# All pairs of the MLPs' odd steps in seven products, two hidden tiles in one buffer, four blocks split by one operation

## The chip, the cores and the metric

The kernel runs on one core of one Trainium2 chip. The metric is the device time of one execution in microseconds, the median of the runs. The engines of the core are named as in the profile: PE (TensorE), with PEld for its weight loads, DVE (VectorE), ACT (ScalarE), POOL (GpSimd) and SP (SyncE, which here only starts the loads of the weights).

## What is computed

A trunk of two layers on a sequence of 256 tokens with 2048 channels, in float32. Layer 0 mixes tokens by a gated short convolution, layer 1 by a stick-breaking attention, and each is followed by an MLP with squared ReLU and 8192 hidden channels:

```
def sq_relu_mlp(u, w_up, w_down):
    return jnp.square(jax.nn.relu(u @ w_up)) @ w_down
...
        u = rmsnorm(h, mlp_pre_g[i])
        h = h + rmsnorm(sq_relu_mlp(u, mlp_w_up[i], mlp_w_down[i]), mlp_post_g[i])
```

The change lies in the two MLPs alone.

## The kernel before

**Numbers in two parts.** A float32 matrix is split into a rounded part (`whi`, `hi`, made by ACT with a copy) and the rest (`wlo`, `lo`, made by DVE with a subtraction), and a product of two such matrices is three matmuls: hi by hi, hi by lo, lo by hi. Weights come from HBM in chunks of 128x1024 float32 (512 KB, tile `raw`, five buffers, loaded by SP's queue one after the other). `chunk(i)` hands out the parts of chunk `i` and first splits all chunks up to `i + 4` (`AHEAD`), so that ACT and DVE work about four chunks ahead of PE. Each part lies in a ring of seven buffers (`RING`).

**Steps and units.** The hidden channels of an MLP are taken in eight steps of 1024 channels, which are eight tiles of 128 channels by 256 tokens (`Hidden(e)`, tiles `n` = 0 to 7, pairs `m` = 0 to 3). In step `e` the kernel computes the hidden tiles of step `e + 1` (`whole_up`, two chunks for each) and multiplies the tiles of step `e` by their rows of the second matrix (`Down.pair`, two chunks for each). One tile up and one pair down take turns; together they are called a unit here, four chunks. A step has eight units: four (`h` = 0) in which the pairs 0, 1, 2, 3 meet one half of the output columns, four (`h` = 1) in which the pairs 1, 2, 3, 0 meet the other half. PE's order is written out by hand; the orders on DVE and ACT are the scheduler's, fixed when the kernel is built.

**Eight products and seven.** A pair down is a product of a 2 by 2 block matrix of the activations (two blocks of 128 tokens, two tiles) with a 2 by 2 block matrix of weights (two chunks, each with two halves of 512 columns). `eight` does it in eight products of 128x512, 24 matmuls, on the two chunks as they are. `seven` does it in seven products, 21 matmuls, by Winograd's form of Strassen's scheme. It needs four sums of the weight blocks (`split_seven`: four DVE subtractions of 128x512 into `sums`, line L210, and then the split into parts of `b11`, of the second chunk, and of two tiles with the sums: names `wloNa` with 512 columns, `wloNb`, `wloNt`, `wloNu` with 1024, N being the chunk's number) and four sums of the activation blocks (`Hidden.sums_of`). The table `SEVEN` says which pairs of a step take seven products: in even steps all four, in odd steps (1, 3, 5) the pairs 1, 2 and 3, and in step 7 only pair 0 in the first half. So pair 0 of an odd step takes eight products, once in each half.

**A hidden tile.** When PE has finished a tile in PSUM, ACT copies one half out (`half`), DVE adds the other (`s<-up,half`, L966, high priority), and ACT applies ReLU and square in place. Before, each tile has a buffer of its own. In a pair that takes seven products, the first tile's first token block is split, then the whole second tile, then the sum `s1`, then the other three sums together (`more`, tag `hg`, five buffers): four copies on ACT and four subtractions on DVE, next to the four sums (`four_sums`, L271) in the tile `sq`, which has one buffer. A pair that takes eight products has both tiles split whole, and the difference of the two token blocks (`dif`) made and split, tile by tile.

The outputs of the products gather in PSUM over all the pairs of a plan; at the plan's end three banks are added by DVE to `mg` (L1073, three operations of 128x512), four are copied out by ACT and added by DMAs that POOL starts (`mg<-more`, L1033).

Of the kernel before, what the change touches and what calls it, by code (L numbers as in the profile page):

```python
# [9 lines left out]
F32 = mybir.dt.float32  # L10
F32R = mybir.dt.float32r
AF = mybir.ActivationFunctionType
ALU = mybir.AluOpType

P = 128
D = 2048
T = 256
NB = T // P
# [28 lines left out]
STEPS = 8  # L47
# [1 line left out]
UP_BANK = 2  # L49
DOWN_BANKS = {(0, 0): 3, (0, 1): 4, (1, 0): 5, (1, 1): UP_BANK, 1: 6, 5: 7, 6: 0, 7: 1}  # L50
LAST_BANKS = [[6, 7], [0, 1]]
SEVEN = [((0, 1, 2, 3),) * 2 if e % 2 == 0 else ((1, 2, 3),) * 2 for e in range(STEPS - 1)] + [((0,), ())]
ORDER = ((0, 1, 2, 3), (1, 2, 3, 0))

IN_N = [j * KD + i for i in range(KD) for j in range(3)]
# [40 lines left out]
def trunk(ctx, tc, x, xT, vecs, rows, ws, out):  # L96
    nc = tc.nc
# [45 lines left out]
    raw, parts, early = {}, {}, {}  # L143
# [109 lines left out]
    def split_tile(xs, k, src):  # L253

        hi, lo = xs[k // 4][:, k % 4, 0, :, :], xs[k // 4][:, k % 4, 1, :, :]
        src = src.rearrange("p (b t) -> p b t", b=NB)
        nc.scalar.activation(hi, src, AF.Copy)
        nc.vector.tensor_tensor(lo, src, hi.bitcast(F32), op=ALU.subtract)
# [7 lines left out]
    def four_sums(to, a11, a21, a12, a22):  # L266
        s1, s2, s3, s4 = to
        for t, v, w, op in (
            (s1, a21, a22, ALU.add), (s2, s1, a11, ALU.subtract), (s3, a11, a21, ALU.subtract), (s4, a12, s2, ALU.subtract),
        ):  # L270
            nc.vector.tensor_tensor(t, v, w, op=op)  # L271
# [25 lines left out]
    def spent(us):  # L297
        clock["us"] += us
        while due and due[0][0] <= clock["us"]:
            heappop(due)[2]()  # L300
# [622 lines left out]
    with tc.tile_pool(name="p_in", bufs=1, reuse_waits="tile") as tmp:  # L923
        y = convolution(tmp)
# [14 lines left out]
    def mlp(pool, i, before, after):  # L939
        u = before.x4  # L940
        part = [[None] * 4 for _ in range(NB)]
        held = {}
        scale = [None] * NB

        def two_parts(parts, src):
            hi, lo = parts
            nc.scalar.activation(hi, src, AF.Copy)
            nc.vector.tensor_tensor(lo, src, hi.bitcast(F32), op=ALU.subtract)

        class Hidden:  # L950


            def __init__(self, e):
                self.xs, self.sums = [None] * (NF // 4), {}
                first, second = SEVEN[e]
                self.pairs = [2 * m for m in first]
                self.apart = [2 * m for m in first if m not in second]
                self.eights = [2 * m for m in range(4) if m not in first] if e < STEPS - 1 else []

            def x(self, n, b):  # L960
                return [part_of(self.xs, n, b, j) for j in range(2)]

            def tile(self, n, ps, half):
                s = pool.tile([P, T], F32, tag="s", name="s", bufs=3)
                with tc.high_priority():
                    nc.vector.tensor_tensor(s[:], ps[:, :T], half[:], op=ALU.add)  # L966
                nc.scalar.activation(s[:], s[:], AF.Relu)  # L967
                nc.scalar.activation(s[:], s[:], AF.Square)
                if self.xs[n // 4] is None:
                    self.xs[n // 4] = operand("hid4")  # L970
                if n in self.pairs and n not in self.apart:
                    two_parts(self.x(n, 0), s[:, :P])
                else:
                    split_tile(self.xs, n, s[:])
                if n in self.pairs:
                    held[n] = s
                elif n - 1 in self.pairs:
                    self.sums[n - 1] = self.sums_of(n - 1, held.pop(n - 1), s)
                elif n - n % 2 in self.eights:
                    if n % 2 == 0:  # L980
                        self.sums[n] = pool.tile([P, 2, 2, P], F32R, tag="d", name="sums", bufs=1)
                    parts = [self.sums[n - n % 2][:, n % 2, j, :] for j in range(2)]
                    d = pool.tile([P, P], F32, tag="dif", name="dif", bufs=1)
                    nc.vector.tensor_tensor(d[:], s[:, :P], s[:, P:], op=ALU.subtract)
                    two_parts(parts, d[:])

            def sums_of(self, n, x, y):

                t = after.dump()
                four_sums([t[:, j * P : (j + 1) * P] for j in range(4)], x[:, :P], x[:, P:], y[:, :P], y[:, P:])  # L990
                if n in self.apart:
                    one = pool.tile([P, 2, 2, P], F32R, tag="d", name="sums", bufs=1)
                    one = [one[:, 0, j, :] for j in range(2)]
                else:
                    one = self.x(n, 1)
                more = pool.tile([P, 6 * P], F32R, tag="hg", name="sums", bufs=5)
                more = [more[:, j * 3 * P : (j + 1) * 3 * P] for j in range(2)]
                two_parts(one, t[:, :P])
                two_parts(more, t[:, P:])
                return [one] + [[m[:, j * P : (j + 1) * P] for m in more] for j in range(3)]  # L1000

        pss, adds = {}, []
# [103 lines left out]
        class Down:  # L1106


            def __init__(self, j, plan):
                self.j, self.plan, self.ps = j, plan, {}  # L1110
                sevens_at = [at for at in plan if at[1] in SEVEN[at[0]][at[2]]]
                whole_at = [at for at in plan if at not in sevens_at and at[0] == STEPS - 1]
# [41 lines left out]
            def eight(self, at, first, xs, n):  # L1154
                ws = [chunk(first + t) for t in range(2)]

                def products(key, own, x, c):
                    self.products(key, own, at, [
                        (x(t), [w[:, c * HALF : (c + 1) * HALF] for w in ws[t]]) for t in range(2)
                    ])  # L1160

                products((0, 0), "sum", lambda t: xs.x(n + t, 0), 0)
                products((1, 0), "sum", lambda t: xs.x(n + t, 1), 0)
                if at[0] == STEPS - 1:
                    products((0, 1), "sum", lambda t: xs.x(n + t, 0), 1)
                    products((1, 1), "whole", lambda t: xs.x(n + t, 1), 1)
                else:
                    products((0, 1), "sum", lambda t: [xs.sums[n][:, t, j, :] for j in range(2)], 1)
                    products(5, "fifth", lambda t: xs.x(n + t, 1), 1)
                spent(4 * UNIT)  # L1170

        for e in range(STEPS):
            for h in range(2):
                for m in SEVEN[e][h]:
                    n = 16 * h + 4 * ORDER[h].index(m) + 2 if e < STEPS - 1 else 8 * h + 2 * m
# [3 lines left out]
        for e in range(STEPS):  # L1179
            first = W["mlp", i, e + 1].base  # L1180
# [303 lines left out]
```

## Time and profile before

| | |
|---|---|
| median of 3 runs (lowest to highest) | 2108.14 us (2107.08 to 2108.43) |
| the profiled execution | 2106.03 us, of which the span from first to last instruction is 2104.3 us |
| granted TensorE clock in it | 0.998 |
| PE busy | 99% of the span |
| DVE busy | 87% |
| ACT busy | 68% |
| chain that ended last | PE 96%, DVE 3% |
| weights `raw<-w_mlp` | 512 issues of 512 KB, 4.7 us each from issue to landing (median) |

In the page a group row gives line, engine, operation, output and input tiles, shapes and count, then the busy time in us and the mean duration in ns, then the idle time of the engine ahead of these instructions. A row of the timeline begins with start and duration in us. A windows row gives, for a stretch of time, the busy time of each engine with its count of instructions, the granted clock, the share of the DMA engines' time and the rate. The steps of the first MLP run from 406 to about 988 us, those of the second from 1470 us on.

### The profile page before, as it was taken

The numbers are of one execution on the slowest core, as the hardware profiler recorded it, in microseconds if no ns is written. First come the engines' busy times: TensorE is split into PE (matmuls) and PEld (weight loads), VectorE is DVE, ScalarE is ACT, GpSimd is POOL, SyncE is SP. The second block draws the span as 40 slices with busy tenths as digits, with TensorE's granted clock in tenths as the row PEclk, the third lists the DMA queues.
The fourth block names the chain that finished last, engine by engine and source line by source line (L and its number), as shares of the span: only waits on it lengthen the run. The fifth ranks groups of instructions, "written<-read, shape, count | busy, mean of one in ns | idle before, by whom it ended". The sixth has DMA issues, their size and how long they took to land.

```text
span 2104.3 us, 29885 instructions
## 1 busy us (share of the span) xinstructions
PE 2089.1 (99%) x10608; PEld 1782.1 (85%) x10608; DVE 1837.6 (87%) x2807; ACT 1437.4 (68%) x2210; POOL 112.9 (5%) x137
## 2 busy tenths in 40 slices
PE   9999999999999999999999999999999999999998
PEld 7888888888888888888888888889888888888886
DVE  8999965999899999999766777558999999999997
ACT  8666544776776776767567888547867767677673
POOL 0000000000100101001000000000001010010010
PEclk9999999999999999999999999999999999999999
DMA  8467674577878868779575555655687687786784
GB/s 291 151 205 250 196 258 143 187 234 229 233 220 233 248 204 244 229 228 257 180 224 168 160 160 161 220 179 171 187 254 227 217 248 221 228 253 208 231 241 162
DMA packets 132342, 449.23 MB, mean 213 GB/s; under 512 B 14816, under 2 KB 15072, under 8 KB 131168
## 3 DMA queue, kind: packets, MB, share of 16 engines
q1 hardware_dynamic: 113184, 406.55, 60.1%
q0 software_dynamic: 18720, 40.38, 9.5%
q8 instruction: 83, 1.36, 0.3%
q14 instruction: 67, 0.55, 0.1%
q10 hardware_dynamic: 288, 0.39, 0.1%
HBM read 413.19 MB, written 2.10 MB: 197 GB/s over the span
## 4 chain that ended last, share of the span: by engine, by line
PE 96%; DVE 3%; issue 0%; DMA 0%; ACT 0%; SPq 0%; DVEq 0%; ACTq 0%
PE up L1013 21%; PE up L1020 12%; PE acc L326 8%; PE acc L328 8%; PE acc L327 8%; PE acc L748 5%; PE more L1127 5%; PE more L1126 5%; PE more L1128 5%; PE acc L1126 5%; PE acc L1127 4%; PE acc L1128 4%; PE lead L748 1%; PE up L1015 1%; PE tr L263 1%; DVE wlo L184 1%
## 5 line engine op out<-in xcount | busy, mean ns | idle before, releaser
L184 DVE TENSOR_TENSOR wlo<-raw,whi 128x1024 fp32r<-128x1024 f32 (+1 forms) x442 | 528.2, 1205 | 96.0 <-ACT whi L173 91.0
L173 ACT ACTIVATE whi<-raw 128x1024 fp32r<-128x1024 f32 (+1 forms) x442 | 454.5, 1044 | 172.8 <-PE acc L328 81.8
L1013 PE MATMUL up<-u,whi 128*128 128x512 f32 x1952 | 464.9, 389 | 0.0
L1013 PEld LDWEIGHTS up<-u,whi 128*128 128x128 f32 x1952 | 365.0, 188 | 74.7
L1020 PEld LDWEIGHTS up<-u,wlo 128*128 128x128 f32 x2048 | 263.6, 191 | 10.3
L1020 PE MATMUL up<-u,wlo 128*128 128x256 f32 x2048 | 268.1, 283 | 0.0
L186 DVE SCALAR_TENSOR_TENSOR wlo<-raw,gv,whi 128x512 fp32r<-128x512 f32 (+1 forms) x160 | 131.8, 854 | 41.4 <-ACT whi L173 40.7
L210 DVE TENSOR_TENSOR sums<-raw,sums 128x512 f32<-128x512 f32 x236 | 161.6, 685 | 1.3
L173 ACT ACTIVATE whi<-raw,gv 128x512 fp32r<-128x512 f32 (+1 forms) x160 | 121.7, 801 | 48.3 <-PE acc L328 41.9
L326 PE MATMUL acc<-whi,u 128*128 128x512 f32 x384 | 153.1, 399 | 0.1
L328 PE MATMUL acc<-whi,u 128*128 128x512 f32 x384 | 149.9, 390 | 0.0
L327 PE MATMUL acc<-wlo,u 128*128 128x512 f32 x384 | 149.7, 390 | 0.0
L1033 POOL DMA_DIRECT2D mg<-more x108 | 94.2, 872 | 829.9 <-ACT more L1088 425.3
L1026 ACT ACTIVATE half<-up 128x256 f32<-128x256 f32 x128 | 48.7, 382 | 99.3 <-PE up L1020 96.2
L748 PE MATMUL acc<-u,whi 128*128 128x512 f32 x416 | 98.9, 391 | 2.7 <-DVE sum L757 2.7
L748 PEld LDWEIGHTS acc<-u,whi 128*128 128x128 f32 x416 | 77.4, 188 | 20.5 <-DVE sum L757 3.7
L210 DVE TENSOR_TENSOR sums<-raw,raw 128x512 f32<-128x512 f32 x118 | 80.8, 685 | 13.8 <-DMA raw<-w_mlp 13.8
L210 DVE TENSOR_TENSOR sums<-raw 128x512 f32<-128x512 f32 x118 | 80.8, 685 | 5.7 <-DMA raw<-w_mlp 5.3
L328 PEld LDWEIGHTS acc<-whi,u 128*128 128x128 f32 x384 | 72.1, 188 | 15.5
L967 ACT ACTIVATE s<-s 128x256 f32<-128x256 f32 x128 | 52.3, 412 | 47.2 <-DVE s L966 45.9
L326 PEld LDWEIGHTS acc<-whi,u 128*128 128x128 f32 x384 | 72.2, 188 | 13.9 <-ACT tk L1316 0.6
L327 PEld LDWEIGHTS acc<-wlo,u 128*128 128x128 f32 x384 | 72.3, 188 | 13.2
(5995 smaller groups left out, 4508.4 us busy)
## 6 DMA issues: line engine op xcount, KB each, us to landing
raw<-w_mlp SPq DMA_DIRECT2D x512, 512.0 KB, 4.7
raw<-w_in SPq DMA_DIRECT2D x94, 512.0 KB, 4.4
mg<-more POOLq DMA_DIRECT2D x108, 256.0 KB, 6.5
raw<-w_out SPq DMA_DIRECT2D x32, 512.0 KB, 4.5
raw<-w_v SPq DMA_DIRECT2D x32, 512.0 KB, 4.4
raw<-w_k SPq DMA_DIRECT2D x32, 512.0 KB, 4.4
raw<-w_q SPq DMA_DIRECT2D x32, 512.0 KB, 4.3
raw<-w_wo SPq DMA_DIRECT2D x32, 512.0 KB, 3.7
```

What stands on the lines that cost most here:

```text
L173: rounded = nc.scalar.activation(hi[:, at], raw[i][:, at], AF.Copy, scale=1.0 if gain is None else gain)
L184: nc.vector.tensor_tensor(lo[:, at], t[:, at], hi[:, at].bitcast(F32), op=ALU.subtract)
L210: nc.vector.tensor_tensor(t, x, y, op=ALU.subtract)
L326: nc.tensor.matmul(ps[:], xh, hi[:, a], start=i == 0 and k == 0, stop=False)
L327: nc.tensor.matmul(ps[:], xh, lo[:, a], start=False, stop=False)
L328: nc.tensor.matmul(ps[:], xl, hi[:, a], start=False, stop=i == self.n - 1 and k == self.ks - 1)
L748: nc.tensor.matmul(ps[:, :cols], w, xs[:, :cols], start=k == 0 and part == parts[0], stop=k == KD - 1 and part == parts[1], skip_group_che ...
L1013: nc.tensor.matmul(ps, weight(0, first, m), x, start=k == 0, stop=False)
L1020: nc.tensor.matmul(pss[n][:, :T], weight(1, first, m), x, start=False, stop=k == KD - 1)
L1126: nc.tensor.matmul(self.ps[key][:], xh, hi, start=first, stop=False)
L1127: nc.tensor.matmul(self.ps[key][:], xh, lo, start=False, stop=False)
L1128: self.done = nc.tensor.matmul(self.ps[key][:], xl, hi, start=False, stop=last)
```

## The change

`SEVEN` now names all four pairs in steps 0 to 6, so twelve pair products (two halves, three odd steps, two MLPs) go from eight products to seven, their chunks through `split_seven`, and their tiles through `sums_of`. The code of the eight-product form for steps other than the last is removed.

The two tiles of a pair share one buffer of 128x2x256 (tag `s`, two buffers in place of three half as large). `sums_of` writes `s1` over the block `a21`, which no product needs, after `s3` has read it. The four blocks that the products need then lie side by side, and one copy on ACT and one subtraction on DVE split all four (128x2x256, 512 elements in each partition). The three other sums are split as before. In step 7 the pair is split as before.

```
-SEVEN = [((0, 1, 2, 3),) * 2 if e % 2 == 0 else ((1, 2, 3),) * 2 for e in range(STEPS - 1)] + [((0,), ())]
+SEVEN = [((0, 1, 2, 3),) * 2] * (STEPS - 1) + [((0,), ())]
...
             def tile(self, n, ps, half):
-                s = pool.tile([P, T], F32, tag="s", name="s", bufs=3)
+                if n % 2 == 0:
+                    held[n] = pool.tile([P, 2, T], F32, tag="s", name="s", bufs=2)
+                both = held[n - n % 2]
+                s = both[:, n % 2, :]
...
-                if n in self.pairs and n not in self.apart:
-                    two_parts(self.x(n, 0), s[:, :P])
-                else:
-                    split_tile(self.xs, n, s[:])
...
-                elif n - n % 2 in self.eights:
...
-                    d = pool.tile([P, P], F32, tag="dif", name="dif", bufs=1)
-                    nc.vector.tensor_tensor(d[:], s[:, :P], s[:, P:], op=ALU.subtract)
-                    two_parts(parts, d[:])
...
+                if n - n % 2 in self.apart or n - n % 2 not in self.pairs:
+                    split_tile(self.xs, n, s)
+                if n % 2:
+                    del held[n - 1]
+                    if n - 1 in self.pairs:
+                        self.sums[n - 1] = self.sums_of(n - 1, both)
...
-                four_sums([t[:, j * P : (j + 1) * P] for j in range(4)], x[:, :P], x[:, P:], y[:, :P], y[:, P:])
...
+                s1 = t[:, 3 * P :] if apart else a21
+                for to, v, w, op in (
+                    (s3, a11, a21, ALU.subtract), (s1, a21, a22, ALU.add),
+                    (s2, s1, a11, ALU.subtract), (s4, a12, s2, ALU.subtract),
+                ):
+                    nc.vector.tensor_tensor(to, v, w, op=op)
...
                 else:
                     one = self.x(n, 1)
+                    hi, lo = (self.xs[n // 4][:, n % 4 : n % 4 + 2, j] for j in range(2))
+                    two_parts((hi, lo), both[:].rearrange("p k (b t) -> p k b t", b=NB))
                 more = pool.tile([P, 6 * P], F32R, tag="hg", name="sums", bufs=5)
                 more = [more[:, j * 3 * P : (j + 1) * 3 * P] for j in range(2)]
-                two_parts(one, t[:, :P])
-                two_parts(more, t[:, P:])
+                two_parts(more, t[:, : 3 * P])
```

On PE, the place is the first pair product of step 1 in the first MLP, its first twelve rows; `whi_4991` and `whi_5019` are its two chunks, `hid` its tiles. Before:

```order
L1126 MATMUL acc<-whi_4991,hid_4220 128x512
L1127 MATMUL acc<-wlo_4992,hid_4220 128x512
L1128 MATMUL acc<-whi_4991,hid_4220 128x512
L1126 MATMUL acc<-whi_5019,hid_4220 128x512
L1127 MATMUL acc<-wlo_5020,hid_4220 128x512
L1128 MATMUL acc<-whi_5019,hid_4220 128x512
L1126 MATMUL acc<-whi_4991,hid_4220 128x512
L1127 MATMUL acc<-wlo_4992,hid_4220 128x512
L1128 MATMUL acc<-whi_4991,hid_4220 128x512
L1126 MATMUL acc<-whi_5019,hid_4220 128x512
L1127 MATMUL acc<-wlo_5020,hid_4220 128x512
L1128 MATMUL acc<-whi_5019,hid_4220 128x512
```

And in the changed kernel, the same place:

```order
L1129 MATMUL more<-whi178a,hid_4200 128x512
L1130 MATMUL more<-wlo178a,hid_4200 128x512
L1131 MATMUL more<-whi178a,hid_4200 128x512
L1129 MATMUL acc<-whi178b,hid_4200 128x512
L1130 MATMUL acc<-wlo178b,hid_4200 128x512
L1131 MATMUL acc<-whi178b,hid_4200 128x512
L1129 MATMUL acc<-whi178b,sums 128x512
L1130 MATMUL acc<-wlo178b,sums 128x512
L1131 MATMUL acc<-whi178b,sums 128x512
L1129 MATMUL more<-whi178t,hid_4200 128x512
L1130 MATMUL more<-wlo178t,hid_4200 128x512
L1131 MATMUL more<-whi178t,hid_4200 128x512
```

Between the tile up ahead of it and the one behind it there stand 24 matmuls before and 21 now; over the whole program PE's list is 36 rows shorter (6471 and 6435), and nothing else on PE changes place.

On DVE, the place is where the weights of that same pair are split, a unit ahead of PE, behind the last weight part of chunk 174; `wlo_4929` and `wlo_4943` are the chunks of the tile up. Before:

```order
L184 TENSOR_TENSOR wlo_4929<-raw_4831,whi_4928 128x1024
L271 TENSOR_TENSOR sq<-s 128x128
L184 TENSOR_TENSOR wlo_4943<-raw_4845,whi_4942 128x1024
L184 TENSOR_TENSOR wlo_4992<-raw_4901,whi_4991 128x1024
L966 TENSOR_TENSOR s<-up,half 128x256
L184 TENSOR_TENSOR wlo_5020<-raw_4903,whi_5019 128x1024
```

Now, from the same place on:

```order
L210 TENSOR_TENSOR sums<-raw_4865 128x512
L210 TENSOR_TENSOR sums<-raw_4867,raw_4865 128x512
L184 TENSOR_TENSOR wlo_4907<-raw_4811,whi_4906 128x1024
L968 TENSOR_TENSOR s<-up,half 128x256
L210 TENSOR_TENSOR sums<-raw_4867,sums 128x512
L184 TENSOR_TENSOR wlo178a<-raw_4865,whi178a 128x512
L210 TENSOR_TENSOR sums<-raw_4867,sums 128x512
L184 TENSOR_TENSOR wlo178b<-raw_4867,whi178b 128x1024
L991 TENSOR_TENSOR s<-s 128x128
L184 TENSOR_TENSOR wlo178t<-sums,whi178t 128x1024
L991 TENSOR_TENSOR sq<-s 128x128
L948 TENSOR_TENSOR hid_4628<-s,hid_4628 128x2x256
```

Two operations for the pair's weights have become eight (four sums, four low parts; `wlo178u` stands just behind these rows), and the hidden pair built at the same time is split by the one operation in the last row.

The third place, on DVE too, is the split of the three sums (`sums<-sq`) of the second pair of `Hidden(1)`, in step 0. Before it stands directly behind the weights of chunk 162:

```order
L184 TENSOR_TENSOR wlo162u<-sums,whi162u 128x1024
L948 TENSOR_TENSOR sums<-sq,sums 128x384
L210 TENSOR_TENSOR sums<-raw_4567 128x512
L210 TENSOR_TENSOR sums<-raw_4569,raw_4567 128x512
L210 TENSOR_TENSOR sums<-raw_4569,sums 128x512
```

Now it stands almost a unit later, among the weights of chunk 166:

```order
L184 TENSOR_TENSOR wlo166a<-raw_4538,whi166a 128x512
L210 TENSOR_TENSOR sums<-raw_4540,sums 128x512
L184 TENSOR_TENSOR wlo166b<-raw_4540,whi166b 128x1024
L948 TENSOR_TENSOR sums<-sq,sums 128x384
L184 TENSOR_TENSOR wlo166t<-sums,whi166t 128x1024
L184 TENSOR_TENSOR wlo166u<-sums,whi166u 128x1024
```

The copy on ACT that goes with it (between `whi166t` and `whi166u` in ACT's list) now waits for PE: `Hidden(0)` still holds four of the five `hg` buffers, pair 0 of `Hidden(1)` has the fifth, and one comes free when PE has used pair 1 in the first unit of the second half. Before, `Hidden(1)` had only three such pairs, and no copy of this kind waits for PE. The same now happens once in each of the steps 0 to 5.

More of the change, by code (lines that the diff above doesn't have):

```diff
@@ L957, in __init__ @@
                 self.apart = [2 * m for m in first if m not in second]
-                self.eights = [2 * m for m in range(4) if m not in first] if e < STEPS - 1 else []
             def x(self, n, b):
@@ L963, in tile @@
             def tile(self, n, ps, half):
-                s = pool.tile([P, T], F32, tag="s", name="s", bufs=3)
+                if n % 2 == 0:
+                    held[n] = pool.tile([P, 2, T], F32, tag="s", name="s", bufs=2)
+                both = held[n - n % 2]
+                s = both[:, n % 2, :]
                 with tc.high_priority():
-                    nc.vector.tensor_tensor(s[:], ps[:, :T], half[:], op=ALU.add)
-                nc.scalar.activation(s[:], s[:], AF.Relu)
-                nc.scalar.activation(s[:], s[:], AF.Square)
+                    nc.vector.tensor_tensor(s, ps[:, :T], half[:], op=ALU.add)
@@ L969, in tile @@
+                nc.scalar.activation(s, s, AF.Relu)
+                nc.scalar.activation(s, s, AF.Square)
                 if self.xs[n // 4] is None:
                     self.xs[n // 4] = operand("hid4")
-                if n in self.pairs and n not in self.apart:
-                    two_parts(self.x(n, 0), s[:, :P])
-                else:
-                    split_tile(self.xs, n, s[:])
[L975 to L978, printed above, removed]
-                elif n - n % 2 in self.eights:
-                    if n % 2 == 0:
-                        self.sums[n] = pool.tile([P, 2, 2, P], F32R, tag="d", name="sums", bufs=1)
-                    parts = [self.sums[n - n % 2][:, n % 2, j, :] for j in range(2)]
-                    d = pool.tile([P, P], F32, tag="dif", name="dif", bufs=1)
-                    nc.vector.tensor_tensor(d[:], s[:, :P], s[:, P:], op=ALU.subtract)
-                    two_parts(parts, d[:])
@@ L987, in sums_of @@
-            def sums_of(self, n, x, y):
-                t = after.dump()
-                four_sums([t[:, j * P : (j + 1) * P] for j in range(4)], x[:, :P], x[:, P:], y[:, :P], y[:, P:])
-                if n in self.apart:
-                    one = pool.tile([P, 2, 2, P], F32R, tag="d", name="sums", bufs=1)
-                    one = [one[:, 0, j, :] for j in range(2)]
+                if n - n % 2 in self.apart or n - n % 2 not in self.pairs:
[4 more added lines that the diff above has]
+                        self.sums[n - 1] = self.sums_of(n - 1, both)
@@ new lines, in sums_of @@
+            def sums_of(self, n, both):
+                t = after.dump()
+                s2, s3, s4 = (t[:, j * P : (j + 1) * P] for j in range(3))
+                a11, a21, a12, a22 = (both[:, j // 2, j % 2 * P : (j % 2 + 1) * P] for j in range(4))
+                apart = n in self.apart
+                s1 = t[:, 3 * P :] if apart else a21
[4 more added lines that the diff above has]
+                    nc.vector.tensor_tensor(to, v, w, op=op)
+                if apart:
+                    one = pool.tile([P, 2, P], F32R, tag="d", name="sums", bufs=1)
+                    one = [one[:, j, :] for j in range(2)]
+                    two_parts(one, s1)
@@ L1163, in eight @@
                 products((1, 0), "sum", lambda t: xs.x(n + t, 1), 0)
[L1164 to L1169, printed above, removed]
+                products((0, 1), "sum", lambda t: xs.x(n + t, 0), 1)
+                products((1, 1), "whole", lambda t: xs.x(n + t, 1), 1)
                 spent(4 * UNIT)
```

## The prediction

> **What bounds the kernel now.** I read the page's shares first, then what PE waited for, then the windows by step and by unit of the first MLP.
>
> ```profile
> span 2104.3 us, 29885 instructions
> PE 2089.1 (99%) x10608; PEld 1782.1 (85%) x10608; DVE 1837.6 (87%) x2807; ACT 1437.4 (68%) x2210; POOL 112.9 (5%) x137
> PE acc L748 <- DVE sum L757: 4.5, 5, 1.7
> ```
>
> PE is busy for 99% of the span, and the longest wait of its list, all of it in the convolution (L748), is 4.5 us in total. So PE's own work sets the time, and the work taken from it counts in full as long as nothing else falls behind. DVE is next. The seven full steps of the first MLP, in windows whose columns are the stretch, its length, then PE, PEld, DVE, ACT and POOL busy:
>
> ```profile
> 406.08:488.72 82.64, 82.64 (x425) 70.90 (x425) 81.34 (x126) 64.50 (x107) 6.99 (x8) 1.00 0.72 211
> 488.72:572.69 83.97, 83.97 (x431) 72.02 (x431) 77.14 (x117) 59.23 (x94) 6.98 (x8) 1.00 0.77 240
> 572.69:655.30 82.61, 82.61 (x425) 70.89 (x425) 80.16 (x116) 61.65 (x93) 6.98 (x8) 1.00 0.77 220
> 655.30:739.27 83.97, 83.97 (x432) 72.02 (x431) 77.90 (x119) 57.15 (x91) 7.85 (x9) 1.00 0.80 239
> 739.27:821.90 82.63, 82.63 (x426) 70.92 (x425) 80.16 (x114) 61.32 (x93) 7.85 (x9) 1.00 0.78 222
> 821.90:905.86 83.96, 83.96 (x431) 72.01 (x431) 77.76 (x119) 56.82 (x90) 7.85 (x9) 1.00 0.79 237
> 905.86:988.50 82.64, 82.64 (x426) 70.92 (x425) 79.98 (x107) 60.49 (x88) 7.88 (x9) 1.00 0.78 224
> ```
>
> PE is busy for every one of these microseconds. An even step takes 82.62 us, an odd one 83.97. DVE has 28.0 us idle in the 582.4 us (the lengths less the 554.4 us busy). By unit, it is all but full wherever seven products run, and rests near the eight-product units:
>
> ```profile
> 488.72:499.72 11.00, 11.00 (x57) 9.42 (x57) 9.76 (x18) 6.49 (x12) 0.00 (x0) 1.00 0.76 283
> 561.68:572.69 11.01, 11.01 (x58) 9.43 (x57) 8.21 (x14) 5.29 (x10) 1.74 (x2) 1.00 1.04 318
> 603.67:614.00 10.33, 10.33 (x54) 8.87 (x54) 10.30 (x15) 7.21 (x11) 0.00 (x0) 1.00 0.72 246
> 624.32:634.65 10.33, 10.33 (x55) 8.87 (x54) 10.33 (x15) 7.36 (x12) 1.74 (x2) 1.00 0.99 244
> ```
>
> **What leaves PE.** An eight-product unit takes 11.00 us, a seven-product one 10.33, so 0.67 to 0.68 for three matmuls. By steps: 83.97 less 82.62 is 1.35 us for an odd step's two units, three odd steps in each of two MLPs, 8.1 us. PE's order is otherwise the same, so nothing else can come from PE.
>
> **What it adds to DVE.** Instructions overlap, so the cost is the distance of starts, not the duration. Rows of stretches in which DVE never rested:
>
> ```profile
> 419.03 1.22 DVE L184 TENSOR_TENSOR wlo150b<-raw,whi150b 128x1024 fp32r<-128x1024 f32 x1
> ...
> 421.30 1.22 DVE L184 TENSOR_TENSOR wlo150u<-sums,whi150u 128x1024 fp32r<-128x1024 f32 x1
> ...
> 423.57 0.42 DVE L966 TENSOR_TENSOR s<-up,half 128x256 f32<-128x256 f32 x1
> ...
> 979.40 0.68 DVE L210 TENSOR_TENSOR sums<-raw 128x512 f32<-128x512 f32 x1
> ...
> 981.81 0.68 DVE L210 TENSOR_TENSOR sums<-raw,sums 128x512 f32<-128x512 f32 x1
> ...
> 402.53 0.55 DVE L948 TENSOR_TENSOR sums<-sq,sums 128x384 fp32r<-128x384 f32 x1
> 403.00 0.28 DVE L948 TENSOR_TENSOR hid<-s,hid 128x128 fp32r<-128x128 f32 x1
> ...
> 404.46 0.42 DVE L258 TENSOR_TENSOR hid<-s,hid 128x256 fp32r<-128x256 f32 x1
> 404.80 0.28 DVE L271 TENSOR_TENSOR sq<-s,sq 128x128 f32<-128x128 f32 x1
> 405.00 0.28 DVE L948 TENSOR_TENSOR hid<-sq,hid 128x128 fp32r<-128x128 f32 x1
> ```
>
> Four of 1024 columns from 419.03 to 423.57: 1.135 us each. Four of 512 from 979.40 to 981.81: 0.60. One of 384: 0.47, of 256: 0.34, of 128: 0.20. A pair's weights cost two of 1024, 2.27 us, in the eight-product form, and five of 512 (four sums, one low part) with three of 1024, 6.41, in the other: 4.14 more, six times in an MLP, 24.8 us. The hidden pair: one operation of 512 (0.60) takes the place of 128, 256 and 128 (0.74), which saves 0.14; a pair that changes form goes from 1.48 (twice 0.34 and two of 0.20) to 1.87 (four of 0.20, 0.60, 0.47). In two neighbouring steps seven pairs save and one pays, 0.6 us saved; in an MLP about 1.8. Net DVE gets 23.0 us more in each MLP and PE 4.05 less.
>
> **Does DVE keep up?** From busy times: 28.0 idle less 23.0 less 4.05 leaves 0.9 us in seven steps, 0.13 a step. From starts: a unit is five of 1024 (5.68), five of 512 (3.00), 0.34 for the tile's addition and half a hidden pair (0.94), 9.95; eight of them and three additions of 0.60 into `mg` make 81.4 of 82.62, 1.2 us a step left. The first is too dark, as busy time counts the full length of an instruction that nothing follows at once; the second knows no waits. Both are above nothing. DVE also has a reserve: it runs ahead of PE.
>
> ```profile
> 425.46 0.39 PE L1127 MATMUL more<-wlo150u,sums 128*128 128x512 f32 x1
> 481.66 1.22 DVE L184 TENSOR_TENSOR wlo174u<-sums,whi174u 128x1024 fp32r<-128x1024 f32 x1
> 487.42 0.39 PE L1127 MATMUL more<-wlo174u,sums 128*128 128x512 f32 x1
> ```
>
> `wlo150u` ended at 422.52 and PE took it at 425.46, 2.9 us ahead, the least of the MLP; `wlo174u`, at the end of a step of seven-product units alone, ended at 482.88 and was taken at 487.42, 4.5 ahead. So a step of this kind builds the reserve up rather than eating it, and I take no stall. With the cover gone, each microsecond that DVE is late past it costs one on PE.
>
> ACT gets 512 and 1024 columns more per changed pair and loses two small copies per hidden pair; in its fullest step it is busy 64.50 of 82.64 us, so nothing on the path. Its copy that now waits for PE has behind it `whi166u` and DVE's `wlo166u`. PE frees the buffer with the sixth of the unit's seven products, 18 matmuls at 0.225 (a third of 0.675), 4.1 us after the tile up; ACT copies that tile out, and then has `whi166a`, `whi166b`, `whi166t` and two small operations to do before the copy that waits. I estimate 0 to 1 us a step on DVE's side, inside the reserve. The loads stay 2 MB a unit, the rate of the even steps.
>
> **The sum.** 2106.03 us of the profiled execution less 8.1 is 2097.9. It lay 2.1 us under the median of 2108.14, and against that the forecast is 2100.0.
>
> **A rule that speaks against the change.** The timeline's rows put the starts of 1024-column operations 1.135 us apart at a duration of 1.22. The Trainium skill, "VectorE: DVE Perf Modes", section "The DRAIN you can't avoid", says that the next operation does not start until the pipe is empty (and exempts one that is not held, in the same section). By the rule alone the durations add up, and the trace does not bear that out. What it would do is the third rival.
>
> **Rivals.**
>
> *1. DVE's waits use up the reserve.* In order, DVE waits for raw weights and for ACT's copies:
>
> ```profile
> DVE sums L210 <- DMA raw<-w_mlp: 8.1, 9, 1.8
> ```
>
> That is for 406 to 988 us. Against it: the units at 603 and 624 rest for 0.03 us at most, and the waits lie where DVE has caught up. For it: an even step rests for 2.45 us (82.61 less 80.16), DVE's share of rest beside the eight-product units is now gone, and the new wait of ACT adds to it. If w is what DVE rests in a step and m the margin (0.13 to 1.2, middle 0.66), six steps lose 6(w - m) and the reserve takes 4.5. With w of 1.4 to 2.0 the stall is 0 to 3.5 us in an MLP, up to 7 in both: 2100 to 2107.
>
> *2. The same on the other side: DVE is the bound.* With w = 2.45 the stall is 6 x 1.79 less 4.5, 6.2 us in an MLP, 12.5 in both, and the time 2112; with the margin of 0.13 it is 9.4 and 18.8, and 2119. I take 2115. Slower than before from a stall of 4.05 in an MLP on, so from w = 2.1 at the middle margin.
>
> *3. DVE's operations do not overlap.* By the mean durations:
>
> ```profile
> L184 DVE TENSOR_TENSOR wlo<-raw,whi 128x1024 fp32r<-128x1024 f32 x434 | 525.2, 1220 | 95.1 <-ACT whi L173 90.3 <-issue 4.8
> L210 DVE TENSOR_TENSOR sums<-raw,sums 128x512 f32<-128x512 f32 x236 | 161.6, 685 | 1.3
> L966 DVE TENSOR_TENSOR s<-up,half 128x256 f32<-128x256 f32 x128 | 53.4, 418 | 0.4
> L948 DVE TENSOR_TENSOR sums<-sq,sums 128x384 fp32r<-128x384 f32 x52 | 28.8, 553 | 4.0 <-ACT sums L947 4.0
> L271 DVE TENSOR_TENSOR sq<-s 128x128 f32<-128x128 f32 x104 | 29.4, 286 | 6.0 <-ACT s L968 5.6
> ```
>
> a unit takes 6.10 + 3.43 + 0.42 + 1.19 = 11.14 us, a step with its additions 91.2, 8.6 over PE; in the six changed steps that is 51 us, and 2151. The even steps would show it already, and PE does not wait in them.
>
> *4. The saving is not on the path:* something with its own pace, the loads or the adding DMAs, holds the odd steps at 83.97 us, and the time stays at 2108. The even steps run at 82.62 with the same bytes and shares of DMA time, which speaks against it. That the products are not saved at all is out: PE's list has 36 matmuls fewer.
>
> **How the numbers follow.** A measurement of this kernel can tell about 0.2%, 4.2 us, from no change. Forecast (stall under 1.5 us): 0.62. Rival 1: 0.17, of which 0.11 still faster by over 4.2 us and 0.06 not. Rival 2: 0.14. Rival 3: 0.01. Rival 4: 0.06. So faster 0.73, same 0.12, slower 0.15. The range goes from 2098.5 (8.1 us and the spread of the runs, some 1.4 us across) through rival 1 to 2108, which also takes in most of rival 4 and leaves out 0.15 above and a little below.
>
> **What would show it.** In the profile after: all seven steps of an MLP at 82.6 us with PE busy throughout and no wait for DVE's low parts; DVE busy about 81 to 82.4 us in each, its rest under 1.5; the least reserve of a `wloNu` 2 us or more; groups of `hid<-s,hid` at 512 columns of about 0.68 us. The forecast is wrong if PE or PEld lists a wait for `wlo` in the MLPs, if odd steps are longer than even ones, or if the reserve falls from step to step.

## The result: 2098.28 us, 10 us less

The changed kernel took 2098.28 us (median of four runs, 2097.94 to 2098.86). The kernel before, measured beside it, took 2108.28 (four runs, 2107.08 to 2112.55). The ratio is 0.9952, with a 95% interval from 0.994 to 0.9965: faster by 0.35 to 0.6%. The forecast was 2100.0, and the range began at 2098.5, so the time lies 0.2 us below it. The gain was larger than the 8.1 us that were forecast, though the interval, some 7 to 13 us, has 8.1 in it.

The profile page of the changed kernel, its first lines:

```profile
span 2097.2 us, 29698 instructions
PE 2082.2 (99%) x10572; PEld 1776.8 (85%) x10572; DVE 1873.6 (89%) x2779; ACT 1450.0 (69%) x2122; POOL 112.6 (5%) x137
```

PE issues 36 matmuls fewer and is still busy for 99% of the span. DVE is busy for 36 us more. The waits of PE in the changed kernel (what it waited for, us in total, times, the longest):

```profile
PE acc L748 <- DVE sum L757: 4.7, 5, 2.0
PE warm L738 <- DVE ones L114: 1.1, 1, 1.1
PE tr L263 <- DVE h L506: 0.3, 1, 0.3
```

That is the whole list. All of it lies outside the MLPs, and there is no wait for a `wlo`. The seven full steps of the first MLP in the changed kernel, by windows with the columns of the prediction's table (length; busy time of PE, PEld, DVE, ACT, POOL; granted clock, DMA share, GB/s), and their sum:

```profile
407.14:489.76 82.62, 82.62 (x425) 70.88 (x425) 82.59 (x123) 63.78 (x96) 6.97 (x8) 1.00 0.74 216
489.76:572.37 82.61, 82.61 (x426) 70.89 (x425) 81.31 (x114) 61.68 (x89) 6.96 (x8) 1.00 0.77 229
572.37:654.98 82.61, 82.61 (x426) 70.89 (x425) 82.25 (x117) 60.35 (x85) 6.96 (x8) 1.00 0.78 230
654.98:737.59 82.61, 82.61 (x426) 70.89 (x425) 81.90 (x116) 60.28 (x85) 7.84 (x9) 1.00 0.81 233
737.59:820.20 82.61, 82.61 (x426) 70.90 (x425) 82.13 (x116) 60.30 (x85) 7.83 (x9) 1.00 0.80 233
820.20:902.82 82.62, 82.62 (x426) 70.90 (x425) 82.14 (x116) 60.31 (x85) 7.83 (x9) 1.00 0.81 233
902.82:985.43 82.61, 82.61 (x426) 70.90 (x425) 79.90 (x109) 59.84 (x88) 7.86 (x9) 1.00 0.79 229
sum 578.29, PE 578.29 PEld 496.26 DVE 572.23 ACT 426.55 POOL 52.24; mean PE 82.61 PEld 70.89 DVE 81.75 ACT 60.94 POOL 7.46
```

Second, fourth and sixth row are the odd steps: 82.61 or 82.62 us where they took 83.97. PE is busy for all of each. DVE is busy for 82.59 of 82.62 us in step 0 and costs PE nothing.

The reserve in the changed kernel, at its least among the sums `u` (timeline: start, duration, engine, line, tiles):

```profile
432.40 1.24 DVE L184 TENSOR_TENSOR wlo154u<-sums,whi154u 128x1024 fp32r<-128x1024 f32 x1
...
436.84 0.39 PE L1130 MATMUL more<-wlo154u,sums 128*128 128x512 f32 x1
```

The low part ended at 433.64 and PE took it at 436.84, 3.2 us later (3.0 in the second MLP). The least over all low parts of a pair's weights is 2.8 us in the first MLP and 2.5 in the second, for a block `b` each time. The reserve then grows: from step 2 on it goes up and down between 5.1 and 8.0 us among the sums `u`, with no fall from one full step to the next before step 6. What DVE waited for in the same steps, and the merged split of the hidden pair among DVE's groups:

```profile
DVE sums L210 <- DMA raw<-w_mlp: 3.3, 6, 0.9
```

```profile
L948 DVE TENSOR_TENSOR hid<-s,hid 128x512 fp32r<-128x512 f32 x27 | 18.7, 691 | 0.0
```

DVE's waits for raw weights, 8.1 us before, are 3.3 now. The merged split takes 0.69 us, and 27 of them stand in these steps.

**Where the 10 us are.** The traces of the two kernels, divided at the same places of the program (us, worked out from the first and last matmuls of each part):

| part | before | after |
|---|---|---|
| up to the first MLP's step 0 | 405.91 | 406.97 |
| steps 0 to 5 (48 units) of the first MLP | 499.79 | 495.71 |
| steps 6 and 7, and all up to the second MLP's step 0 | 564.71 | 564.69 |
| steps 0 to 5 (48 units) of the second MLP | 499.79 | 495.71 |
| steps 6 and 7, and all to the end | 134.10 | 134.09 |

Each MLP gives 4.08 us, together 8.16. That is the whole of what the change does in these two traces. The first row cost the changed kernel 1.06 us more in this execution; there PE's list is the same in both, and the last 48.3 us of it, the hidden tiles made ahead of step 0, take the same time in both, so the difference arose ahead of the MLP. So the pair of profiled executions differs by 7.2 us (2106.03 and 2098.86), the medians by 10.0.

### The profile page after: what moved, and what is told of

Its sections match the earlier page's. It is cut to its first block, busy times and chain, and to the rows that moved or that the text cites. A ratio compares the mean times of both kernels' runs of the same rounds, so it can differ in the third digit from the quotient of the medians.

```text
span 2097.2 us, 29698 instructions
## 1 busy us (share of the span) xinstructions
PE 2082.2 (99%) x10572; PEld 1776.8 (85%) x10572; DVE 1873.6 (89%) x2779; ACT 1450.0 (69%) x2122; POOL 112.6 (5%) x137
## 3 DMA queue, kind: packets, MB, share of 16 engines
q8 instruction: 83, 1.36, 0.3%
## 4 chain that ended last, share of the span: by engine, by line
PE 96%; DVE 3%; issue 0%; DMA 0%; ACT 0%; SPq 0%; DVEq 0%; ACTq 0%
PE up L1016 21%; PE up L1023 12%; PE acc L326 8%; PE acc L328 8%; PE acc L327 8%; PE acc L748 5%; PE more L1130 5%; PE more L1129 5%; PE more L1131 5%; PE acc L1129 4%; PE acc L1130 4%; PE acc L1131 4%; PE lead L748 1%; PE up L1018 1%; PE tr L263 1%; DVE wlo L184 1%
## 5 line engine op out<-in xcount | busy, mean ns | idle before, releaser
L184 DVE TENSOR_TENSOR wlo<-raw,whi 128x1024 fp32r<-128x1024 f32 (+1 forms) x418 | 502.0, 1211 | 85.5 <-ACT whi L173 85.0
L173 ACT ACTIVATE whi<-raw 128x1024 fp32r<-128x1024 f32 (+1 forms) x418 | 430.2, 1044 | 177.8 <-PE acc L328 81.0
L1023 PEld LDWEIGHTS up<-u,wlo 128*128 128x128 f32 x2048 | 263.6, 191 | 10.3
L210 DVE TENSOR_TENSOR sums<-raw,sums 128x512 f32<-128x512 f32 x260 | 180.5, 694 | 0.9
L210 DVE TENSOR_TENSOR sums<-raw,raw 128x512 f32<-128x512 f32 x130 | 90.4, 696 | 4.5 <-DMA raw<-w_mlp 4.5
L210 DVE TENSOR_TENSOR sums<-raw 128x512 f32<-128x512 f32 x130 | 90.5, 697 | 2.8 <-DMA raw<-w_mlp 2.5
L748 PEld LDWEIGHTS acc<-u,wlo 128*128 128x128 f32 x416 | 53.3, 193 | 3.8 <-DVE sum L757 2.2
```

The source lines that it names most:

```text
L173: rounded = nc.scalar.activation(hi[:, at], raw[i][:, at], AF.Copy, scale=1.0 if gain is None else gain)
L184: nc.vector.tensor_tensor(lo[:, at], t[:, at], hi[:, at].bitcast(F32), op=ALU.subtract)
L210: nc.vector.tensor_tensor(t, x, y, op=ALU.subtract)
L748: nc.tensor.matmul(ps[:, :cols], w, xs[:, :cols], start=k == 0 and part == parts[0], stop=k == KD - 1 and part == parts[1], skip_group_che ...
L1023: nc.tensor.matmul(pss[n][:, :T], weight(1, first, m), x, start=False, stop=k == KD - 1)
```

## The experiments

The theory: PE is the bound in both kernels, its 36 matmuls fewer are worth 8.1 us, and DVE's added work disappears in its rest and its reserve. The rivals: the merged split or the new buffers speed something up, or the gain contains something beside the matmuls. In the expectations A is the theory, B a part of the gain that comes from elsewhere, C the merged split and D more room on DVE than was reckoned.

**1. The table alone, and the split alone.** `seven_only` changes one line of the kernel before:

```diff
-SEVEN = [((0, 1, 2, 3),) * 2 if e % 2 == 0 else ((1, 2, 3),) * 2 for e in range(STEPS - 1)] + [((0,), ())]
+SEVEN = [((0, 1, 2, 3),) * 2] * (STEPS - 1) + [((0,), ())]
```

> The table SEVEN alone is changed; tiles keep their own buffers and the four blocks their three splits. DVE gets 0.14 us more per hidden pair than in the changed kernel, 0.56 us a step, which leaves 0.6 of the 1.2 us a step reckoned from starts. Theory A (DVE keeps up by itself): no stall, the same time as the changed kernel within 1 us. Rival C (the merged split is what makes room): the reserve falls from step to step and PE waits for wlo, 2 to 8 us over the changed kernel.

It took 2098.35 us (2097.46 to 2101.11), ratio 0.9955 [0.9943, 0.9968]. Windows of its first MLP, steps 1 and 3 and the sum of seven:

```profile
489.76:572.37 82.61, 82.61 (x425) 70.89 (x424) 82.25 (x122) 62.51 (x98) 6.96 (x8) 1.00 0.79 232
...
654.98:737.59 82.61, 82.61 (x425) 70.89 (x424) 82.55 (x124) 60.90 (x93) 7.84 (x9) 1.00 0.79 234
...
sum 578.29, PE 578.29 PEld 496.23 DVE 575.69 ACT 431.20 POOL 53.11; mean PE 82.61 PEld 70.89 DVE 82.24 ACT 61.60 POOL 7.59
```

The same steps with DVE 3.5 us busier in seven of them. Its least reserve was 2.0 us for a block `b` and 2.5 for a `u`. So the table alone gives the whole gain in the MLPs. The merged buffer spares DVE some 0.5 us a step, which this kernel does not need.

`merged_only` does the reverse: tiles merged and split by one operation, the table as before.

```diff
-                s = pool.tile([P, T], F32, tag="s", name="s", bufs=3)
+                if n % 2 == 0:
+                    held[n] = pool.tile([P, 2, T], F32, tag="s", name="s", bufs=2)
+                both = held[n - n % 2]
+                s = both[:, n % 2, :]
...
-                    d = pool.tile([P, P], F32, tag="dif", name="dif", bufs=1)
+                    d = after.dump()[:, :P]
```

> The other half of the change alone: two tiles in one buffer and one split for four blocks, with eight products kept for pair 0 of the odd steps (the difference that they need lies in the buffer of the sums). PE's list is that of the kernel before. Theory A: the time of the kernel before, 2106 to 2108, as DVE's 0.14 us a hidden pair were never waited for; PE waits in no step. Theory B (the merged split is what removes PE's occasional waits for DVE in the MLPs): 1 to 2 us faster than the kernel before.

2108.40 us (ten runs, 2105.86 to 2109.67) against 2107.47 of the kernel before beside it; ratio 1.0 [0.9991, 1.001]. By itself the split gives nothing that these runs can tell, although DVE has 8 us less to do in the span. It fits a kernel in which only PE's work counts.

**2. PE's share without DVE's.** `cut_product` is the kernel before with the second factor of the fifth product left out in the twelve eight-product pairs; that part of the result is missing. It takes the 36 matmuls from PE and adds nothing to DVE.

```diff
-                    products(5, "fifth", lambda t: xs.x(n + t, 1), 1)
+                    self.products(5, "fifth", at, [(xs.x(n, 1), [w[:, HALF:] for w in ws[0]])])
```

> The kernel before, with one of the eight products left out in the twelve pairs that take eight (a part of the computation is missing), so PE does 36 matmuls fewer and DVE nothing more. Theory A: 8.1 us under the kernel before, the same as the changed kernel within 1 us. Theory B: between, as part of the 10 us came from elsewhere in the change: about 2 us slower than the changed kernel.

2099.51 us (2098.67 to 2103.97), ratio 0.9963 [0.995, 0.9975]. Windows of its steps 0 and 1:

```profile
411.97:494.61 82.64, 82.64 (x427) 70.90 (x425) 81.75 (x126) 64.85 (x108) 6.97 (x8) 1.00 0.71 213
494.61:577.22 82.61, 82.61 (x425) 70.89 (x424) 76.01 (x115) 58.82 (x94) 6.96 (x8) 1.00 0.77 240
```

The odd step has 6.6 us of rest on DVE and lasts 82.61 us, as with a full DVE. Its two MLPs take 495.71 us each, the number of the changed kernel to the hundredth. So what DVE does more costs nothing, and the matmuls alone give the 4.08 us of each MLP.

**3. How much more DVE could take.** Both kernels are the changed one with the fourth sum of a weight pair computed twice, 0.60 us by the start distances: in every second pair of the MLPs (`dose_half`, 2.4 us a step) or in every pair (`dose_full`, the condition without its second half, 4.8 us a step).

```diff
             nc.vector.tensor_tensor(t, x, y, op=ALU.subtract)
+        if i >= 146 and i // 4 % 2 == 0:
+            nc.vector.tensor_tensor(t4, b21, t2, op=ALU.subtract)
```

> The changed kernel, with one of the four weight sums done twice in every second pair product: 0.60 us more on DVE, four times a step, 2.4 us a step. Theory A (margin of 1.2 us a step less some waits, reserve of about 4 us): over by 1.2 to 2.0 us a step, in seven steps 8 to 14, less 4 of reserve, so 4 to 10 us of PE waiting for wlo in each MLP, 2106 to 2118. Rival D (DVE has more room than reckoned, its busy time stretches to fill the step): no wait, 2098.

> The same in every pair product: 4.8 us more on DVE in a step. Theory A: over by 3.6 to 4.4 us a step, 25 to 31 in seven steps, less 4 of reserve, 21 to 27 in each MLP: 2140 to 2152, and DVE busy without a rest. Rival D: under 2110.

`dose_half` took 2129.45 us (2125.47 to 2130.48), ratio 1.0097 [1.0081, 1.0114]; `dose_full` 2153.65 (2153.33 to 2156.55), ratio 1.022 [1.0205, 1.0235]. Both are above what was expected, the first by 11 us. Windows of steps 3 and 4 of the first MLP with the half dose, and of steps 2 and 3 with the full one:

```profile
656.17:741.10 84.93, 83.84 (x426) 70.56 (x425) 84.83 (x122) 57.49 (x84) 7.84 (x9) 1.00 0.82 228
741.10:827.10 86.00, 84.19 (x425) 70.27 (x424) 83.82 (x119) 60.05 (x86) 7.84 (x9) 1.00 0.79 224
```

```profile
575.80:662.70 86.90, 84.86 (x425) 70.06 (x425) 86.74 (x124) 57.62 (x85) 6.97 (x8) 1.00 0.77 218
662.70:749.60 86.90, 84.86 (x425) 70.05 (x424) 86.70 (x124) 57.18 (x84) 7.84 (x9) 1.00 0.79 220
```

With the full dose a step is DVE's own length: 86.9 us, 86.7 of it busy (step 4 took 87.8). Less the dose of 4.8 that is 81.9 to 82.1 us of DVE's own work, 0.5 to 0.7 us below PE's 82.61. The prediction's middle margin was 0.66. With the half dose the reserve carries steps 0 to 2 at 82.6 us. Then PE waits, and the steps take 84.9, 86.0 and 85.5 us where 82.6 less 0.66 plus 2.4 would make 84.3. Part of the difference stands in DVE's list of waits for those three steps (656 to 912 us, one row). The row below it is the largest of the rows in which PE waits for a low part, over the whole span:

```profile
DVE s L993 <- ACT s L972: 2.5, 2, 1.5
```

```profile
PE acc L1132 <- DVE wlo L184: 2.6, 2, 1.3
```

In the three steps DVE is busy for 252.9 us, 84.3 a step as reckoned, and idle for 3.5, of which 2.5 are these two waits for ACT's square. In the same steps ACT waits for DVE in turn (11.5 us for the sum `s1`). Without a reserve such waits come on top. The expectation left them out. It also counted only the seven full steps. From the seventh step to the last down matmul of the MLP the stretch took 132.3 and 132.6 us, against 125.7 and 125.2 in the changed kernel, about 7 us more each time, and 3.7 of these lie behind the last tile up, in the last pair of the seventh step and in step 7. So rival 2 of the prediction, DVE as the bound, does come about with more work: it begins somewhere between 0.5 us more on DVE a step (`seven_only`) and 2.4.

**4. One more pair.** `more7` gives the second pair of step 7 seven products as well, and one more buffer for it:

```diff
-SEVEN = [((0, 1, 2, 3),) * 2] * (STEPS - 1) + [((0,), ())]
+SEVEN = [((0, 1, 2, 3),) * 2] * (STEPS - 1) + [((0, 1), ())]
...
-                    one = pool.tile([P, 2, P], F32R, tag="d", name="sums", bufs=1)
+                    one = pool.tile([P, 2, P], F32R, tag="d", name="sums", bufs=2)
```

> The changed kernel, with pair 1 of step 7 in seven products too (its sum s1 kept apart, in a second buffer of the kind that pair 0 has). PE does three matmuls fewer in each MLP, 0.68 us each, and DVE 4.1 us more at a place where it is 3 to 5 us ahead. Theory A: 1.4 us under the changed kernel, seen in the trace as the length of step 7, too little for the times to tell. Rival: step 7's reserve doesn't hold it, PE waits for wlo, and the time is the same or up to 3 us more.

2097.43 us (2096.84 to 2099.38), ratio to the kernel before 0.9952 [0.9937, 0.9967]. In its trace the stretches that hold step 7 take 0.64 and 0.63 us less than in the changed kernel (564.05 and 133.46 us), six matmuls in all, 1.3 us where 1.4 was expected. The page of that kernel:

```profile
span 2095.0 us, 29710 instructions
PE 2080.1 (99%) x10566; PEld 1774.2 (85%) x10566; DVE 1882.0 (90%) x2803; ACT 1454.6 (69%) x2130; POOL 112.8 (5%) x137
```

It is the shortest trace here. By the total times alone it cannot be told from the changed kernel, since it differs by about the spread of the runs; the saving is shown by the two stretches.

**5. The same two kernels again.** The medians differ by 10.0 us and the MLPs by 8.16. To see what else differs, the kernel before (`base`, `base2`, `base3`, `base4`) and the changed one (`again`, `again2`) ran once more, without an edit.

> The kernel before, once more. Theory A: the change is worth its matmuls, 8.1 us, and the other 1.9 us of the measured 10.0 lie in the level of the kernel before: its executions differ by what the granted clock does (the profile after shows 3.4 us at half clock near 43 us), so single executions here lie between 2106 and 2109, those near 2106 with a mean clock of 0.998 or more and no other loss, and a trace without a wait of PE in the MLPs. Theory B: the kernel before loses about 2 us in most executions to waits of PE for DVE's low parts that the profiled one happened not to have; then the trace of an execution near 2108 shows PE or PEld waiting for wlo in the MLPs.

> The changed kernel, once more. Theory A: 8.1 us under the fastest executions of the kernel before on the same chip, so 2097.9 plus at most 1.5 where the clock was halved for some microseconds. Theory B: 10 us under the kernel before in every round.

> One more trace of the kernel before, for the step lengths and for what precedes the first MLP. Theory A alone: steps of 82.6 and 84.0 us to the hundredth in both MLPs, all the difference between executions ahead of the first MLP (clock at half, late first loads). Theory B in its small form (the eight-product units leave DVE short of loaded weights, and a tile's addition stands behind them): in some of these traces a step next to an eight-product unit is 0.2 to 1.4 us longer, with PE waiting for DVE's s.

> The same, a further execution. Theory A alone: nothing in the steps. Theory B in its small form: over all the traces of kernels with eight-product units about 0.5 us a trace on the mean.

> The same, a further execution. Theory A alone: nothing in the steps. Theory B in its small form: about 0.5 us a trace on the mean.

> One more trace of the changed kernel. Both theories: all steps 82.61 to 82.64 us; what varies lies ahead of the first MLP.

`base`: 2108.76 us (eleven runs, 2106.40 to 2110.71) beside 2108.19 (fifteen runs of the same kernel). `again`: 2099.25 (five, 2097.64 to 2101.06), ratio 0.996 [0.9947, 0.9972]. The single profiled executions: 2109.11, 2106.15 and 2106.30 for `base2` to `base4`, 2098.15 for `again2`. Divided as in the table above, with `middle` and `rest` for its third and fifth part, all twelve traces without a dose (us):

| kernel | up to step 0 | first MLP | middle | second MLP | rest |
|---|---|---|---|---|---|
| before | 405.91 | 499.79 | 564.71 | 499.79 | 134.10 |
| base | 408.38 | 499.79 | 564.69 | 501.15 | 134.10 |
| base2 | 407.41 | 499.79 | 564.71 | 501.40 | 134.10 |
| base3 | 405.99 | 499.79 | 564.71 | 499.83 | 134.10 |
| base4 | 405.91 | 499.79 | 564.74 | 500.07 | 134.10 |
| merged_only | 409.40 | 499.79 | 564.73 | 499.95 | 134.08 |
| after | 406.97 | 495.71 | 564.69 | 495.71 | 134.09 |
| again | 407.23 | 495.71 | 564.71 | 495.71 | 134.10 |
| again2 | 406.22 | 495.71 | 564.72 | 495.71 | 134.10 |
| seven_only | 405.56 | 495.71 | 564.71 | 495.71 | 134.08 |
| cut_product | 411.97 | 495.71 | 564.69 | 495.71 | 134.09 |
| more7 | 406.13 | 495.71 | 564.05 | 495.71 | 133.46 |

Two things vary. Up to step 0 of the first MLP, where PE's list is the same in all, the traces differ by up to 6.4 us (405.56 to 411.97); the last 48.3 us of that part are equal in all, so it happens ahead of the MLP. And in the second MLP the kernels with eight-product units lose between nothing and 1.6 us (mean 0.58 over six traces), those without them nothing in six traces. In `base`, 1.1 of the 1.36 us lost are one wait of PE, shown from its list of waits and from the timelines of DVE and of PE around it (start, duration, tiles, and in brackets the idle time before and its releaser):

```profile
PE up L1013 <- DVE s L966: 1.1, 1, 1.1
```

```profile
1633.20 0.69 DVE L210 TENSOR_TENSOR sums<-raw 128x512 f32<-128x512 f32 x1 [0.20 <-DMA raw<-w_mlp]
...
1635.55 0.69 DVE L210 TENSOR_TENSOR sums<-raw,raw 128x512 f32<-128x512 f32 x1 [1.66 <-DMA raw<-w_mlp]
...
1640.24 0.41 DVE L966 TENSOR_TENSOR s<-up,half 128x256 f32<-128x256 f32 x1
```

```profile
1639.25 0.39 PE L1128 MATMUL more<-whi,hid 128*128 128x512 f32 x1
...
1640.71 1.65 PE L1013 MATMUL up<-u,whi 128*128 128x512 f32 x6 [1.07 <-DVE s L966]
```

A raw chunk landed late and DVE stood still for 1.66 us before the sums of the next pair's weights. Behind those sums in DVE's order came the addition that empties PE's bank for `up`, and PE waited for it, not for a `wlo`. In `base2` the same wait is 1.3 us of the 1.61 lost; the smaller losses of the other traces are in no wait that the list has. In `again2` DVE waited for raw chunks for 0.5 us in the window of 1560 to 1645 us, in `base` for 5.7. Such waits of DVE are not rare: in the second MLP they add up to 9.6 to 13.6 us in the six traces with eight-product units and to 0.9 to 1.7 in those with the new table. But `cut_product`, which splits its weights as the kernel before does, has 9.8 us of them and loses nothing on PE. Why one of them reaches PE in some executions is not shown, and six traces of each are few.

## Why the prediction was right, and where it was not

**What leaves PE: right.** 8.1 us were forecast and 8.16 measured; odd steps at 82.6 us, PE busy throughout. `cut_product` shows that the matmuls are the cause, and `seven_only` that the table is.

**Does DVE keep up: right.** The margin of 0.13 to 1.2 us a step, middle 0.66, is 0.5 to 0.7 by the full dose. The sum of busy times was the dark one, as the prediction said: it left 0.9 us idle in seven steps, and 6.1 were measured, since DVE's busy time rose by 17.8 us in place of 23.0. DVE's rest per step was forecast under 1.5 and was 0.0 to 1.3 in steps 0 to 5 (2.7 in step 6, whose successor has fewer sums to build). The least reserve of a `u` was to be 2 us or more and was 3.2 and 3.0 in the two MLPs. The 2.9 us that the prediction calls the least of the MLP before is the least of the sums `u`; its block `wlo150b` had 2.5. There was no stall.

**The new wait of ACT:** put at 0 to 1 us a step on DVE's side, inside the reserve. It cost nothing that the profile lists: ACT has no wait of this copy for PE, and DVE's three waits for ACT in the seven steps (1.4 us in all) are for `whi` parts of chunks 146 and 194 and of a tile up. PE did not wait in either MLP in the three traces of the changed kernel.

**Rivals 1, 2 and 4** did not come about: no PE wait for a `wlo`, and the odd steps are shorter by what PE lost. Rival 3 needs DVE's durations to add up. Six operations of the changed kernel's timeline, in a row, show that they do not:

```profile
599.84 0.69 DVE L210 TENSOR_TENSOR sums<-raw,sums 128x512 f32<-128x512 f32 x1
600.44 0.69 DVE L184 TENSOR_TENSOR wlo222a<-raw,whi222a 128x512 fp32r<-128x512 f32 x1
601.04 1.23 DVE L184 TENSOR_TENSOR wlo222b<-raw,whi222b 128x1024 fp32r<-128x1024 f32 x1
602.17 1.23 DVE L184 TENSOR_TENSOR wlo222t<-sums,whi222t 128x1024 fp32r<-128x1024 f32 x1
603.31 1.23 DVE L184 TENSOR_TENSOR wlo222u<-sums,whi222u 128x1024 fp32r<-128x1024 f32 x1
604.44 0.29 DVE L991 TENSOR_TENSOR sq<-s 128x128 f32<-128x128 f32 x1
```

The starts are 0.60 us apart behind 512 columns and 1.13 to 1.14 behind 1024, as in the rows of before, with durations of 0.69 and 1.23. The rule of the Trainium skill ("VectorE: DVE Perf Modes", "The DRAIN you can't avoid"), that the next operation does not start until the pipe is empty, does not fit these rows; the exception that the same section makes, that an operation which is not held starts earlier, does.

**The sum: the failed step.** The working gave 2097.9 (2106.03 less 8.1). As the profiled execution "lay 2.1 us under the median", the text then added these 2.1 and put the forecast at 2100.0, with the range's low end about one spread (1.4) below it, at 2098.5, above its own sum. Four executions of the changed kernel gave 2097.94 to 2098.86: they start at the sum, not at the median less 8.1. The low end should have been at 2097 or below, as a median of three cannot be known to better than the 1.4 us of their spread, and the sum itself must lie inside. How near it was is chance: the miss of 0.2 us is smaller than the spread, and the same kernel run again (`again`) took 2099.25, inside the range.

**"Nothing else can come from PE": probably wrong by a little.** The traces with eight-product units lose 0.58 us on average in the second MLP (section 5), which the profiled execution of before did not, and none of the traces without such units does. If that holds beyond these twelve traces, the change is worth about 8.7 us, an estimate (8.16 and 0.58). Over all executions of the two kernels in these measurements, with those of `seven_only` (43 of before, 14 of the changed work), the medians are 2108.18 and 2098.60, a difference of 9.6 us (8.5 to 10.3 by resampling, more than one chip mixed). Some 0.8 us of that are not accounted for. The part ahead of the first MLP differs between traces of one and the same kernel by more than this (405.91 to 408.38 for the kernel before), so chance is likely, but that is not shown.

## What to carry to other kernels

Here PE all but never waited in the MLPs, and each matmul that went was worth its issue distance (36 times 0.227 us), whatever happened on the engines beside it. That ended when one of those had more work in a step than PE (with the half dose, DVE's 84.3 us against 82.6). How near that is can't be read from a busy share (DVE busy for 82.59 of a step's 82.62 us cost nothing): add up the start distances of one unit, and measure the reserve from the end of a part to its first use. A forecast that starts from the profiled execution and one that starts from the median of three runs differed here by 2.1 us. The range has to hold both, and both are uncertain by the spread of the runs.

## What the runs showed of the hardware

**A brief half clock after short rests.** Five of the twelve traces without a dose have a stretch of 3.4 us in which PE's granted clock is a half, early in the program (43 to 48 us). The same window of `base`, then of before (windows, columns as above):

```profile
44.50:47.90 3.40, 3.40 (x12) 2.82 (x12) 3.40 (x8) 1.43 (x3) 0.00 (x0) 0.51 0.67 234
```

```profile
44.50:47.90 3.40, 3.40 (x18) 2.79 (x17) 3.40 (x9) 2.42 (x5) 0.00 (x0) 1.00 0.77 247
```

Twelve matmuls instead of 18 in the same time. Just ahead of the stretch PE was idle for 1.7 to 2.0 us. But all twelve traces have such a rest there (1.9 us in `again` and `seven_only`), and in seven of them no half clock follows; what decides it is not shown. Three of the five are in kernels with eight-product units and two in others. One of those (`cut_product`) has a second stretch at 276 us, behind a wait of 2.0 us; both are part of why its profiled execution is the longest of its runs (2103.97 us). The kernel before itself has the stretch in two of its five traces, so this belongs to the spread and not to the change.

**Work over the margin cost more than its excess.** A dose of 2.4 us a step, 1.7 over DVE's middle margin, took up to 3.4 us of a step from PE (86.0 against 82.6). With the reserve gone, DVE's waits for ACT, 2.5 us in three steps, were paid too.
